# A streaming encoder layer on one core: the sums of x in two heads' slots, the row scale's chain behind the heads, and two kinds of transfer on GpSimd's queue

## The chip, the core and the metric

The kernel runs on one core of one Trainium2 chip. The core has a matrix engine (TensorE, called PE in the profile, PEld for its weight loads), a vector engine (DVE), a scalar engine (ACT), GpSimd (POOL), and SP, which here only issues DMAs. Each engine works through its own queue in order; a DMA is issued from the queue of an engine (here SP or POOL, a few from ACT) and is carried out by 16 DMA engines that all queues share. The metric is the device time of one execution in microseconds; lower is better.

## What is computed

One step of one layer, for 512 prompt frames and 64 sample frames, so 576 columns everywhere in the kernel:

```python
hn = rmsnorm(x, g_norm1)
proj = hn @ w_in
q, k, v, gb, gc, hc = jnp.split(proj, [ATTN_W, 2 * ATTN_W, 3 * ATTN_W, 3 * ATTN_W + CONV_CH, 3 * ATTN_W + 2 * CONV_CH], axis=-1)
q = rmsnorm(q.reshape(B, T, N_HEADS, HEAD_DIM), g_q)
k = rmsnorm(k.reshape(B, T, N_HEADS, HEAD_DIM), g_k)
o_attn = stick_breaking_blocks(q, k_all, v_all, P).reshape(B, T, ATTN_W)
u = gc * hc
conv = conv_w[0] * padded[:, 0:T] + conv_w[1] * padded[:, 1:T + 1] + conv_w[2] * padded[:, 2:T + 2]
o_conv = gb * conv
mix = jnp.concatenate([rmsnorm(o_attn, g_attn_out), rmsnorm(o_conv, g_conv_out)], axis=-1)
x = x + mix @ w_out
h2 = rmsnorm(x, g_norm2)
x = x + (jax.nn.silu(h2 @ w_gate) * (h2 @ w_up)) @ w_down
```

The model width is 2048, there are 8 heads of 128, 8 convolution groups of 128 channels, and the feed-forward width is 5632. The outputs are y, the new keys and values, and the new convolution state, all in 32-bit floats.

## The kernel before

Everything is kept with channels on the 128 partitions and the 576 frames along the free axis, in two halves of 288. A product of 32-bit precision is three matmuls: each operand is split into a high part (a cast, ScalarE, line 223 or 176) and a low part (a subtraction, VectorE, line 224 or 177), and high x high, low x high and high x low are added up in PSUM.

**The order of the work.** TensorE's order is the written one (`tc.manual_schedule`, line 111). The orders of the other engines' queues, SP's and POOL's among them, are made by the framework's planner, except at the start and in the last feed-forward part, where they are the written ones too. Work that has to come between other work is a generator in `pipe` (class `Pipeline`, line 66): each k-step of a product, three matmuls, is one tick, and `yield n` lets a generator sleep for n ticks. `flush` runs all that is left, without any spacing.

**The heads.** `head(h)` projects q, k and v for a head (six products of 16 k-steps, 96 ticks) and spawns the norms, the attention and at its end `put_mix`, which splits a half of the head's output, adds its squares to `acc_a` on GpSimd and stores high and low part to `mix_dram`. The eight outputs lie in `o_attn`, one slot of 576 columns a head.

**The sums of x.** The convolution's inner products, six of eight groups, use a scheme with seven products in place of eight, and need sums of blocks of the scaled x. `x_sums` (line 526), spawned behind head 0, makes them during the heads: for each of 8 pairs j of k-blocks it loads x from `xt_dram` into the slots of heads 6 and 7, which are not used yet, scales and combines four quarters into the slots of heads 4 and 5, and stores the four results in two puts: each put splits two of them into the one buffer `xs_out` and stores both to `xs_dram`, with 8 ticks between the puts of a pair. A pair takes 20 + 3 + 8 + 8 + 8 = 47 ticks, eight pairs 376.

**The row scale.** `group_scale` (line 514) turns the summed squares of the heads, `acc_a`, into the scale by which the first half of the output projection is multiplied: for each half a split, two matmuls with ones (`ssg`, lines 468 and 469), then `rsqrt_mean`. It is spawned at the end of the last head's `attend` with a delay of 4 ticks.

**Stage B.** `open_b` (line 782) is called when the third product of the first convolution group has its first half; it flushes all generators, frees the heads' tiles and starts to load three of the four sums into `bt["pool"]`'s tiles `t1` to `t3`. Two groups run as plain products, the other six in 9 calls of seven products (`conv_run`), each operand prepared four products ahead (`conv_prepare`). The two halves of a group's output go through `put_mix` as well, into places 8 to 15 of `mix_dram`. In the last call, product 6 is the last to read tile `t1` and product 7 the last to read `t2`; behind each, one half of the heads' `mix_dram` is loaded into the freed tile as `ma[0]` and `ma[1]` (line 983). Products 5, 3 and 4 of that call follow, then the output projection: for each of 16 row blocks and both halves, 8 k-steps over the heads (`pjo`), first half 0 and then half 1, so `ma[0]` and then `ma[1]` are read whole within the first two products. Each weight block of 1024 KB is loaded and split ahead of its use (`load_weight`, `split_weight`), and the 16 blocks of x, 288 KB each, are loaded for the residual. Then come the convolution groups' half, and the feed-forward part.

The launch reserves 1024 bytes per partition for GpSimd's DMAs (`dynamic_dma_scratch_size=1024`, line 1626). Before the change POOL's queue issues DMAs only late in the kernel: 7 stores of `hid_dram` and 32 loads of the residual that accumulate (line 1508).

Of the kernel before, what the change touches and what calls it, by code (L numbers as in the profile page):

```python
# [10 lines left out]
F32 = mybir.dt.float32  # L11
F32R = mybir.dt.float32r
AF = mybir.ActivationFunctionType
ALU = mybir.AluOpType
# [6 lines left out]
HALF = T // 2  # L21
# [3 lines left out]
NH = 8  # L25
# [69 lines left out]
def tile_hybrid_stream_step(  # L95
# [6 lines left out]
    nc = tc.nc  # L102
# [21 lines left out]
    xt_dram = tc.dram_tile([KD, P, T], F32, name="xt_dram")  # L124
# [3 lines left out]
    xs_dram = tc.dram_tile([4, NP, 2, P, HALF], F32, name="xs_dram")  # L128
    mix_dram = tc.dram_tile([2, KD, 2, P, HALF], F32, name="mix_dram")
# [79 lines left out]
    pipe = Pipeline()  # L209
# [12 lines left out]
    def split(hi, lo, src, lo_eng=None):  # L222
        nc.scalar.copy(out=hi, in_=src)  # L223
        (lo_eng or nc.vector).tensor_tensor(out=lo, in0=src, in1=hi.bitcast(F32), op=ALU.subtract)  # L224
# [35 lines left out]
    def misc(name):  # L260
        return ps_z.tile([P, 512], F32, tag="misc", name=name, bufs=2)
# [40 lines left out]
    o_attn = apool.tile([P, NH, T], F32, tag="oa", name="o_attn")  # L302
# [69 lines left out]
    with tc.manual_schedule(engines={mybir.EngineType.Activation, mybir.EngineType.DVE, mybir.EngineType.SP}):  # L372
        raw, raw3, src = weight_raw(0)
# [25 lines left out]
        for kt in range(KD + LAG):  # L399
# [66 lines left out]
    def channel_sums(src_hi, src_lo, a, b, name):  # L466
# [33 lines left out]
    def put_mix(k, i, src, gcol, acc, first):  # L500

        t = tmp.tile([P, 2, HALF], F32R, tag="hl", name="mx")
        nc.scalar.activation(out=t[:, 0], in_=src, func=AF.Copy, scale=gcol)
        if first:
            nc.scalar.activation(out=acc, in_=src, func=AF.Square)
        else:
            sq = tmp.tile([P, HALF], F32, tag="sq", name="sqm")
            nc.scalar.activation(out=sq, in_=src, func=AF.Square)
            nc.gpsimd.tensor_tensor(out=acc, in0=acc, in1=sq, op=ALU.add)
        nc.vector.scalar_tensor_tensor(out=t[:, 1], in0=src, scalar=gcol, in1=t[:, 0].bitcast(F32),  # L510
                                       op0=ALU.mult, op1=ALU.subtract)
        nc.sync.dma_start(out=mix_dram[i, k].rearrange("f p t -> p f t"), in_=t.bitcast(F32))

    def group_scale(acc, dst, rows_of):

        for a, b in HALVES:
            sh, sl = parts("sqg")
            split(sh, sl, acc[:, a:b])
            yield rows_of
            ss = channel_sums(sh, sl, a, b, "ssg")  # L520
            rsqrt_mean(dst[:, a:b], ss, 8 * P, HALF)
            yield rows_of

    acc_a = rpool.tile([P, T], F32, tag="R", name="acc_a", bufs=2)

    def x_sums():


        for j in range(NP):
            raw = o_attn[:, 6:8, :]  # L530
            nc.sync.dma_start(out=raw, in_=xt_dram[2 * j : 2 * j + 2].rearrange("k p t -> p k t"))
            yield 20
            ev, od = raw[:, 0, :], raw[:, 1, :]
            ge, go = g1c[:, 2 * j : 2 * j + 1], g1c[:, 2 * j + 1 : 2 * j + 2]
            ta, tb = (o_attn[:, q, :].rearrange("p (q t) -> p q t", q=2) for q in (4, 5))
            b11, b22 = tb[:, 0], ta[:, 1]
            nc.scalar.activation(out=b11, in_=ev[:, :HALF], func=AF.Copy, scale=ge)
            nc.scalar.activation(out=b22, in_=od[:, HALF:], func=AF.Copy, scale=go)
            nc.vector.scalar_tensor_tensor(out=ta[:, 0], in0=ev[:, HALF:], scalar=ge, in1=b11,
                                           op0=ALU.mult, op1=ALU.subtract)  # L540
            nc.vector.scalar_tensor_tensor(out=tb[:, 0], in0=ev[:, HALF:], scalar=ge, in1=b22,
                                           op0=ALU.mult, op1=ALU.subtract)
            yield 3
            nc.vector.tensor_tensor(out=ta[:, 1], in0=b22, in1=ta[:, 0], op=ALU.subtract)
            nc.vector.scalar_tensor_tensor(out=tb[:, 1], in0=od[:, :HALF], scalar=go, in1=ta[:, 1],
                                           op0=ALU.mult, op1=ALU.subtract)
            for q, two in ((0, ta), (2, tb)):
                yield 8
                split(xs_out[:, :, 0, :], xs_out[:, :, 1, :], two)
                for r in range(2):  # L550
                    nc.sync.dma_start(out=xs_dram[q + r, j].rearrange("f p t -> p f t"), in_=xs_out[:, r].bitcast(F32))
            yield 8

    lags = [0]

# [45 lines left out]
    def attend(h, st):  # L601
# [78 lines left out]
        yield 16  # L680
        vtok, vh, vl = st["vtok"], st["vh"], st["vl"]
        po = misc("po")
        mm(po[:, 384:512], vtok[:, 3, :], pb[3], start=True, stop=False, skip_group_check=True)
        for i in (2, 1, 0):
            for n, (a_, b_) in enumerate(((vh, ph[i]), (vl, ph[i]), (vh, pl[i]))):
# [10 lines left out]
        for b in (2, 1, 0):  # L696
            nc.gpsimd.tensor_tensor(out=sums[:, b * TS : (b + 1) * TS], in0=sums[:, (b + 1) * TS : (b + 2) * TS],
                                    in1=sp[:, (b + 1) * TS : (b + 2) * TS], op=ALU.add)
# [11 lines left out]
                                       op0=ALU.min, op1=ALU.add)  # L710
# [7 lines left out]
        for i, (a, b) in enumerate(HALVES):  # L718
            yield 3
            put_mix(h, i, o_attn[:, h, a:b], col("ga", h), acc_a[:, a:b], h == 0)  # L720
        if h == NH - 1:
            pipe.spawn(group_scale(acc_a, acc_a, 30), 4)

    def values(h, st, Ev):
        yield 5
# [56 lines left out]
    def open_b():  # L782

        pipe.flush()
        t1.release()
        bt["pool"] = bpool = tc.alloc_tile_pool(name="bpool", bufs=1, reuse_waits="tile", side="left")
        for q in (1, 2, 3):
            t = bt[q] = bpool.tile([P, NP, 2, HALF], F32R, tag=f"t{q}", name=f"xs_t{q}")
            nc.sync.dma_start(out=t.bitcast(F32), in_=xs_dram[q].rearrange("j f p t -> p j f t"))
        cx = apool.tile([P, NH * T], F32, tag="oa", name="cx")  # L790
        bt["raw"] = cx[:, :2048]
        bt["s1"] = cx[:, 2048:3072].rearrange("p (j c) -> p j c", c=P)
        bt["c"] = cx[:, 3072 : 3072 + UW - 2]
        bt["acc"] = cx[:, 3072 + UW : 3072 + UW + T]

    uc = cpool.tile([P, UC], F32, tag="uc", name="uc")
    u = uc[:, :UW]
# [177 lines left out]
    ma = {}  # L975
    for k_, (n, p_) in enumerate(corder):
        conv_run(n, p_)
        if k_ + 4 < len(corder):
            conv_prepare(*corder[k_ + 4])
        if n == len(CU) - 1 and p_ in (6, 7):  # L980
            i = p_ - 6
            ma[i] = bt["pool"].tile([P, NH, 2, HALF], F32R, tag=f"t{p_ - 5}", name=f"mixa{i}")
            nc.sync.dma_start(out=ma[i].bitcast(F32), in_=mix_dram[i, :NH].rearrange("k f p t -> p k f t"))
        if k_ in (len(corder) - 6, len(corder) - 4):
            load_weight()
        if k_ == len(corder) - 3:
            split_weight(nc.vector)
# [651 lines left out]
```

## Time and profile before

| | us |
|---|---|
| median of 3 runs | 2419.79 |
| lowest, highest | 2417.83, 2422.32 |
| the profiled execution | 2421.78 |
| its span | 2420.1 |

| stage (from the timeline) | about, us |
|---|---|
| turning x, start of head 0 | 0 to 45 |
| heads | 45 to 465 |
| convolution groups, plain and in calls | 430 to 716 |
| output projection | 717 to 924 |
| first feed-forward block | 924 to 999 |
| gate and up | 999 to 1900 |
| down | 1900 to 2420 |

The profiled execution's own time stands 1.99 us above the median. A row of a view by stretches gives the stretch, its length, the busy time and instructions of each engine, the clock that TensorE was granted, the share of the DMA engines' time, and GB/s. A timeline row gives the start, how long, the engine and line, the operation, output and inputs, and in brackets the idle time before and what ended it. A waits row gives who waited for whom, the sum of the waits, their number and the longest. In the list of DMA issues the last number is the median time from issue to landing.

### The profile page before, as it was taken

How to read it: one execution, taken by the hardware profiler on the slowest of the kernel's cores; microseconds unless marked ns; L12 is line 12 of the kernel's file. 1: busy time of each engine (PE TensorE's matmuls, PEld its weight loads, DVE VectorE, ACT ScalarE, POOL GpSimd, SP SyncE). 2: the span in 40 equal slices, each digit the busy share in tenths (PEclk: the TensorE clock that was granted, in tenths of full speed). 3: DMA queues.
4: the chain of work that ended last, by engine and by line, in shares of the span. 5: the costliest groups of instructions: out<-in, count | busy, mean ns of one | idle time of the engine just before them, and what ended most of it. 6: DMA issues, size and time to landing. Idle time of an engine off the chain costs nothing.

```text
span 2420.1 us, 44077 instructions
## 1 busy us (share of the span) xinstructions
PE 2389.3 (99%) x17921; PEld 2376.1 (98%) x17921; DVE 1865.9 (77%) x2810; ACT 1137.6 (47%) x2015; POOL 236.2 (10%) x336
## 2 busy tenths in 40 slices
PE   8999999999999999999999999999999999999999
PEld 8999999999999999999999999999999999999999
DVE  7877666568875567888888888888888777887876
ACT  6666655424442245444444444444444444444444
POOL 1111111100100020000000000000000001431211
PEclk9999999999999999999999999999999999999999
DMA  8555333554357342553444444434534945885542
GB/s 282 167 173 163 92 93 104 175 161 125 92 193 251 98 136 90 154 159 117 151 149 139 134 144 149 145 124 154 159 114 155 323 148 179 235 234 194 196 134 80
DMA packets 500739, 378.96 MB, mean 157 GB/s; under 512 B 11582, under 2 KB 490680, under 8 KB 500536
## 3 DMA queue, kind: packets, MB, share of 16 engines
q1 hardware_dynamic: 494648, 369.04, 47.7%
q0 software_dynamic: 5168, 6.79, 1.6%
q8 instruction: 140, 2.29, 0.4%
q14 instruction: 63, 0.52, 0.1%
q10 hardware_dynamic: 720, 0.33, 0.0%
HBM read 292.93 MB, written 83.18 MB: 155 GB/s over the span
## 4 chain that ended last, share of the span: by engine, by line
PE 87%; DVE 5%; DMA 4%; ACT 3%; issue 1%; POOL 0%; SPq 0%; ACTq 0%; POOLq 0%; DVEq 0%
PE psy L1389 32%; PE psw L1389 16%; PE pj L214 10%; PE pjo L214 8%; PE psx L1389 8%; PE psy L910 5%; PE psw L910 2%; PE pw L1232 2%; PE psx L910 1%; DMA xs_dram<-xs_out 1%; DVE wlo L177 1%; DMA mixa<-mix_dram 1%; DVE whl L224 1%; DMA raw_a<-in_w_in_dram 1%; DMA o_attn<-xt_dram 0%
## 5 line engine op out<-in xcount | busy, mean ns | idle before, releaser
L1389 PE MATMUL psy<-t,whl 128*128 128x288 f32 x2916 | 437.9, 295 | 0.0
L1389 PE MATMUL psy<-h_s,whl 128*128 128x288 f32 x2724 | 411.3, 295 | 2.7 <-ACT part L1399 2.7
L224 DVE TENSOR_TENSOR whl<-raw_a,whl 128x1024 fp32r<-128x1024 f32 (+4 forms) x324 | 355.9, 1100 | 66.9 <-ACT whl L223 66.0
L1389 PEld LDWEIGHTS psy<-t,whl 128*128 128x128 f32 x2916 | 403.3, 188 | 0.2
L214 PE MATMUL pj<-x,whi 128*128 128x288 f32 x1856 | 401.3, 301 | 0.3 <-DVE x L355 0.3
L1389 PEld LDWEIGHTS psy<-h_s,whl 128*128 128x128 f32 x2724 | 377.8, 188 | 3.5 <-ACT part L1399 3.4
L1389 PE MATMUL psw<-t,whl 128*128 128x288 f32 x2592 | 376.8, 295 | 0.0
L223 ACT CAST whl<-raw_a 128x1024 fp32r<-128x1024 f32 (+4 forms) x324 | 296.8, 919 | 164.6 <-issue 38.7
L1389 PEld LDWEIGHTS psw<-t,whl 128*128 128x128 f32 x2592 | 354.0, 188 | 0.2
L214 PEld LDWEIGHTS pj<-x,whi 128*128 128x128 f32 x1856 | 309.8, 191 | 1.1 <-DVE x L355 0.7
L214 PE MATMUL pj<-x,wlo 128*128 128x288 f32 x928 | 276.3, 298 | 0.1
L224 DVE TENSOR_TENSOR whl<-raw_b,whl 128x1024 fp32r<-128x1024 f32 (+5 forms) x186 | 193.9, 1043 | 68.9 <-ACT whl L223 68.0
L223 ACT CAST whl<-raw_b 128x1024 fp32r<-128x1024 f32 (+5 forms) x186 | 160.9, 867 | 161.4 <-issue 69.5
L1399 ACT COPY part<-psy 128x288 f32<-128x288 f32 x237 | 94.7, 399 | 268.4 <-PE psy L1389 268.1
L214 PEld LDWEIGHTS pj<-x,wlo 128*128 128x128 f32 x928 | 176.9, 191 | 0.7 <-DVE wlo L422 0.3
L1389 PE MATMUL psx<-h_s,whl 128*128 128x288 f32 x1122 | 165.1, 295 | 0.2 <-DVE gs L1212 0.2
L1389 PEld LDWEIGHTS psx<-h_s,whl 128*128 128x128 f32 x1122 | 154.2, 188 | 0.4 <-ACT form L223 0.4
L176 ACT CAST whi<-raw_a 128x1024 fp32r<-128x1024 f32 (+1 forms) x101 | 101.7, 1028 | 95.5 <-PE pjo L214 64.2
L177 DVE TENSOR_TENSOR wlo<-raw_a,whi 128x1024 fp32r<-128x1024 f32 (+1 forms) x96 | 119.6, 1264 | 8.7 <-ACT whi L176 5.5
L223 ACT CAST whl<-s 128x1024 fp32r<-128x1024 f32 (+5 forms) x79 | 70.1, 887 | 98.7 <-PE psw L1389 97.2
L214 PE MATMUL pjo<-mixa,whi 128*128 128x288 f32 x512 | 102.6, 295 | 2.9 <-DMA mixa<-mix_dram 2.9
L214 PE MATMUL pjo<-mixc,whi 128*128 128x288 f32 x512 | 101.7, 294 | 0.0
(421 smaller groups left out, 3885.6 us busy)
## 6 DMA issues: line engine op xcount, KB each, us to landing
hid_dram<-form SPq DMA_DIRECT2D x147, 288.0 KB, 2.6
raw_a<-in_w_in_dram SPq DMA_DIRECT2D x41, 1024.0 KB, 5.5
raw_a<-in_w_gate_dram SPq DMA_DIRECT2D x23, 1024.0 KB, 5.3
raw_a<-in_w_up_dram SPq DMA_DIRECT2D x23, 1024.0 KB, 5.5
raw_b<-in_w_gate_dram SPq DMA_DIRECT2D x21, 1024.0 KB, 7.2
raw_b<-in_w_up_dram SPq DMA_DIRECT2D x21, 1024.0 KB, 6.4
h_s<-hid_dram SPq DMA_DIRECT2D x10, 2016.0 KB, 9.8
raw_a<-in_w_out_dram SPq DMA_DIRECT2D x16, 1024.0 KB, 5.1
```

Source lines behind the costliest of these rows:

```text
L176: nc.scalar.copy(out=hi[:, a:b], in_=raw[:, a:b])
L177: lo_eng.tensor_tensor(out=lo[:, a:b], in0=raw[:, a:b], in1=hi[:, a:b].bitcast(F32), op=ALU.subtract)
L214: mm(ps, w_[:, k, csl], x_, start=(k == 0 and n == 0), stop=(k == nk - 1 and n == 2))
L223: nc.scalar.copy(out=hi, in_=src)
L224: (lo_eng or nc.vector).tensor_tensor(out=lo, in0=src, in1=hi.bitcast(F32), op=ALU.subtract)
L910: mm(ps, whl[:, w_, j, :], x_, start=(start and j == 0 and q == 0), stop=(j == NP - 1 and q == 2), skip_group_check=True)
L1232: mm(pss[j, i], w_[:, k, j * P : (j + 1) * P], x_, start=(kk == 0 and k == 0 and n == 0), stop=(kk == 1 and k == 7 and n == 2))
L1389: mm(ps, whl[:, w_, j, :], x_, start=(start and j == 0 and q == 0), stop=(j == len(xs_) - 1 and q == 2), skip_group_check=True)
L1399: nc.scalar.copy(out=t, in_=st["y"])
```

## The change

It has three parts.

1. `x_sums` works in place: the four quarters of a pair are combined in the slots of heads 6 and 7 themselves, one operation every 8 ticks, and the slots of heads 4 and 5 are left alone. The first put stands between the second and the third combination and the second at the end, 24 ticks apart; a pair takes 18 + 7 x 8 = 74 ticks, eight pairs 592. An assertion says that heads 6 and 7 write their slots only after the last pair.
2. `group_scale` for `acc_a` is spawned at the end of `open_b`, behind the flush, instead of at the end of the last head.
3. The convolution groups' stores in `put_mix` go by GpSimd's queue; so do the loads of `ma`, each in four pieces of two heads (576 KB) instead of one load of 2304 KB on SP's queue.

```diff
-        nc.sync.dma_start(out=mix_dram[i, k].rearrange("f p t -> p f t"), in_=t.bitcast(F32))
+        (nc.sync if k < NH else nc.gpsimd).dma_start(out=mix_dram[i, k].rearrange("f p t -> p f t"), in_=t.bitcast(F32))
...
+        four = o_attn[:, 6:8, :].rearrange("p k (i t) -> p (k i) t", i=2)
+        b11, b12, b21, b22 = (four[:, q, :] for q in range(4))
+        stt, tt = nc.vector.scalar_tensor_tensor, nc.vector.tensor_tensor
+        def put(two, names):
+            split(xs_out[:, :, 0, :], xs_out[:, :, 1, :], two)
+            for r, q in enumerate(names):
+                nc.sync.dma_start(out=xs_dram[q, j].rearrange("f p t -> p f t"), in_=xs_out[:, r].bitcast(F32))
         for j in range(NP):
-            raw = o_attn[:, 6:8, :]
-            nc.sync.dma_start(out=raw, in_=xt_dram[2 * j : 2 * j + 2].rearrange("k p t -> p k t"))
-            yield 20
+            nc.sync.dma_start(out=o_attn[:, 6:8, :], in_=xt_dram[2 * j : 2 * j + 2].rearrange("k p t -> p k t"))
+            yield 18
...
-            for q, two in ((0, ta), (2, tb)):
-                yield 8
-                split(xs_out[:, :, 0, :], xs_out[:, :, 1, :], two)
-                for r in range(2):
-                    nc.sync.dma_start(out=xs_dram[q + r, j].rearrange("f p t -> p f t"), in_=xs_out[:, r].bitcast(F32))
+            nc.scalar.activation(out=b11, in_=b11, func=AF.Copy, scale=ge)
+            nc.scalar.activation(out=b22, in_=b22, func=AF.Copy, scale=go)
             yield 8
+            stt(out=b11, in0=b12, scalar=ge, in1=b11, op0=ALU.mult, op1=ALU.subtract)
+            yield 8
+            stt(out=b12, in0=b12, scalar=ge, in1=b22, op0=ALU.mult, op1=ALU.subtract)
+            yield 8
+            put(four[:, 0:2, :], (0, 2))
+            yield 8
+            tt(out=b22, in0=b22, in1=b11, op=ALU.subtract)
+            yield 8
+            stt(out=b21, in0=b21, scalar=go, in1=b22, op0=ALU.mult, op1=ALU.subtract)
+            yield 8
+            put(four[:, 2:4, :], (3, 1))
+            yield 8
+        free_places.append(True)
...
+        assert h < 6 or free_places
...
-        if h == NH - 1:
-            pipe.spawn(group_scale(acc_a, acc_a, 30), 4)
...
         bt["acc"] = cx[:, 3072 + UW : 3072 + UW + T]
+        pipe.spawn(group_scale(acc_a, acc_a, 30), 4)
...
-            nc.sync.dma_start(out=ma[i].bitcast(F32), in_=mix_dram[i, :NH].rearrange("k f p t -> p k f t"))
+            for k in range(0, NH, 2):
+                nc.gpsimd.dma_start(out=ma[i][:, k : k + 2].bitcast(F32),
+                                    in_=mix_dram[i, k : k + 2].rearrange("k f p t -> p k f t"))
```

More of the change, by code (lines that the diff above doesn't have):

```diff
@@ L531, in x_sums @@
-            nc.sync.dma_start(out=raw, in_=xt_dram[2 * j : 2 * j + 2].rearrange("k p t -> p k t"))
-            yield 20
-            ev, od = raw[:, 0, :], raw[:, 1, :]
+            nc.sync.dma_start(out=o_attn[:, 6:8, :], in_=xt_dram[2 * j : 2 * j + 2].rearrange("k p t -> p k t"))
+            yield 18
             ge, go = g1c[:, 2 * j : 2 * j + 1], g1c[:, 2 * j + 1 : 2 * j + 2]
-            ta, tb = (o_attn[:, q, :].rearrange("p (q t) -> p q t", q=2) for q in (4, 5))
-            b11, b22 = tb[:, 0], ta[:, 1]
@@ L537, in x_sums @@
[L537 to L546, printed above, removed]
-            for q, two in ((0, ta), (2, tb)):
-                yield 8
-                split(xs_out[:, :, 0, :], xs_out[:, :, 1, :], two)
-                for r in range(2):
-                    nc.sync.dma_start(out=xs_dram[q + r, j].rearrange("f p t -> p f t"), in_=xs_out[:, r].bitcast(F32))
@@ L554, in tile_hybrid_stream_step @@
+            yield 8
[4 more added lines that the diff above has]
+        free_places.append(True)
+    free_places = []
     lags = [0]
```

## Prediction

> **What bounds the kernel now.** I read the page first, then busy time by stretches, the waits of the matmul queue, and the timelines around each wait.
>
> ```profile
> PE 2389.3 (99%) x17921; PEld 2376.1 (98%) x17921; DVE 1865.9 (77%) x2810; ACT 1137.6 (47%) x2015; POOL 236.2 (10%) x336
> ```
> ```profile
> 145.00:195.00 50.00, 48.93 (x365) 48.12 (x364) 38.06 (x73) 29.82 (x65) 8.47 (x13) 1.00 0.58 181
> 245.00:295.00 50.00, 50.00 (x376) 49.63 (x376) 33.72 (x66) 29.58 (x65) 7.59 (x14) 1.00 0.33 98
> 445.00:470.00 25.00, 22.34 (x161) 21.37 (x160) 11.46 (x20) 10.54 (x20) 4.01 (x13) 1.00 0.46 137
> 470.00:520.00 50.00, 50.00 (x369) 50.00 (x368) 27.07 (x42) 13.90 (x21) 3.67 (x7) 0.97 0.77 256
> 520.00:600.00 80.00, 80.00 (x607) 80.00 (x607) 64.11 (x83) 34.48 (x47) 5.58 (x14) 1.00 0.36 108
> 705.00:740.00 35.00, 31.58 (x235) 30.84 (x234) 20.52 (x38) 9.49 (x17) 2.90 (x4) 1.00 1.01 355
> ```
> ```profile
> 120.00:130.00 10.00, 7.20 (x31) 6.67 (x32) 8.59 (x15) 7.72 (x17) 2.59 (x5) 0.59 0.58 168
> 130.00:140.00 10.00, 10.00 (x72) 10.00 (x72) 3.49 (x8) 4.43 (x10) 0.73 (x1) 0.90 0.63 198
> ```
>
> Columns of the last two fences: stretch, its length, busy time of PE, PEld, DVE, ACT and POOL, granted clock, DMA share, GB/s. TensorE is busy 2389.3 of the 2420.1 us, so nothing off its path matters until it makes it wait, and a cure can win only gaps and slow clock. Three gaps touch the change: the first heads, where the sums of x run (idle in 145 to 195, none in 245 to 295, after the sums); 2.7 us before 470; and 3.4 us around 717. A gap also costs clock: 0.59 and 0.90 over the 20 us after one gap are 4.1 + 1.0 = 5.1 us, and 0.97 over 470 to 520 is 1.5 us.
>
> **Part 1, the sums of x.** The same matmul falls at the same place of each head, so its spacing is the length of a head.
>
> ```profile
> 76.83 0.60 PE L739 MATMUL kc<-ident,cK 128*128 128x128 f32 x4
> 134.96 0.60 PE L739 MATMUL kc<-ident,cK 128*128 128x128 f32 x4
> 238.39 0.60 PE L739 MATMUL kc<-ident,cK 128*128 128x128 f32 x4
> 287.85 0.60 PE L739 MATMUL kc<-ident,cK 128*128 128x128 f32 x4
> ```
> ```profile
> 109.17 6.50 DMA xs_dram<-xs_out
> 115.75 0.69 ACT xs_out L223
> ```
> ```profile
> PE vta L586 <- DVE Ev L768: 2.5, 2, 2.1
> PE pjo L214 <- DMA mixa<-mix_dram: 2.9, 2, 2.4
> PE ssg L468 <- ACT sqg L223: 2.1, 2, 1.5
> ```
> ```profile
> xs_dram<-xs_out SPq DMA_DIRECT2D x32, 288.0 KB, 5.2
> o_attn<-xt_dram SPq DMA_DIRECT2D x8, 576.0 KB, 5.5
> ```
>
> A head without the sums takes 287.85 - 238.39 = 49.46 us. The three before it took 58.13 and 103.43, so 161.56 - 3 x 49.46 = 13.2 us too much. The biggest piece is the stall near 120 with its slow clock. In the chain of waits the second put of a pair found the one `xs_out` buffer still being stored (6.50 us), ScalarE stood before it, and the head's own work queued behind. The two puts lay 8 ticks apart; a tick is 49.46 / 96 = 0.515 us, so 4.1 us against a landing of 5.2. Now they lie 24 ticks apart, 12.4 us, and a pair takes 18 + 7 x 8 = 74 ticks instead of 47: eight pairs are 592 ticks, 6.2 heads. The operations are the same four on VectorE, two on ScalarE and two splits, so no work is removed; the assertion in `attend` issues nothing. VectorE in a quiet head is busy 33.72 of 50; 38.06 with the sums. Spread by 47/74, the extra 4.3 becomes some 2.8, which stays under the 38.06 that left 1.1 us idle. The load gets 18 ticks (9.3 us) instead of 20, against a landing of 5.5; it now waits for the last split of the pair, which ordered SP's queue ahead of it anyway. If this cover goes, ScalarE stands again, now in six heads. Bounds: a gain of 13.2, and a loss of 3 (half the 1.1 us idle in each of the six). I take a gain of **9**: the stall and the clock at 120 (2.1 + 5.1), and about a third of the other 6.
>
> **Part 2, row scale's chain.**
>
> ```profile
> 465.11 0.39 PE L716 MATMUL os<-ws,vtok 128*128 128x128 f32 x2
> 467.02 0.40 PE L468 MATMUL ssg<-sqg,oner 128*128 128x288 f32 x1 [1.52 <-ACT sqg L223]
> 469.60 0.30 PE L214 MATMUL pj<-x,whi 128*128 128x288 f32 x1
> ```
>
> Opening stage B empties the list of pending generators at once, so in TensorE's hand-written order the four sums of `acc_a` stand right behind the last head's `os`, before their splits are made. Spawned after the emptying, each has 30 ticks between its split and its matmuls. From 465.5 (end of `os`) to 469.6 is 4.1 us; the four matmuls come back later at 3.17 / 24 = 0.13 us each (24 take 3.17, rows of part 4), 0.5; so 3.6, and the 1.5 us of slow clock behind it: a gain of **5.1**, bounds 3.0 and 5.1. Its VectorE and ScalarE work falls into 470 to 520, where they are busy 27 and 14 of 50; its result is first used after 717. Were that cover gone, the same 4.1 would only move.
>
> **Part 3, the conv groups' stores by GpSimd.** Sixteen stores leave SP and cost POOL an issue each, 0.73 us (rows below), 12 us on an engine 10% busy. TensorE has no gap in 520 to 600, so nothing can be won. Behind a store that waits for VectorE's low part stand POOL's adds and its clears of `u`; the buffer comes free later, with the next product's high part on ScalarE behind it. I take 0, bounds 0 and 6 (2 us late for each of three pairs of groups).
>
> **Part 4, the output projection's input.** This decides.
>
> ```profile
> 686.50 18.57 SPq L184 DMA_DIRECT2D raw_a<-in_w_out_dram  x2
> 706.93 3.93 SPq L983 DMA_DIRECT2D mixa<-mix_dram  x2
> ```
> ```profile
> 699.91 3.17 PE psy L910 x24
> 703.08 3.17 PE psw L910 x24
> 717.05 0.40 PE L214 MATMUL pjo<-mixa,whi 128*128 128x288 f32 x1 [0.53 <-DMA mixa<-mix_dram]
> ```
> ```profile
> 1922.54 0.73 POOL L1152 DMA_DIRECT2D hid_dram<-acc_ax  x1 [2.66 <-DVE acc_ax L224]
> 1925.16 0.73 POOL L1152 DMA_DIRECT2D hid_dram<-form  x1 [1.90 <-DVE acc_z L1414]
> 1927.45 0.73 POOL L1152 DMA_DIRECT2D hid_dram<-acc_z  x1 [1.56 <-DVE acc_t L1414]
> ...
> 2056.89 2.73 POOL L1508 DMA_DIRECT2D acc<-x_dram  x3
> 2063.33 0.86 POOL L1508 DMA_DIRECT2D acc<-x_dram  x1 [3.71 <-issue]
> ...
> 2112.17 2.64 POOL L1508 DMA_DIRECT2D acc_z<-x_dram  x3
> 2115.74 0.86 POOL L1508 DMA_DIRECT2D acc_z<-x_dram  x1 [0.93 <-issue]
> ```
> ```profile
> hid_dram<-form POOLq DMA_DIRECT2D x3, 288.0 KB, 5.7
> hid_dram<-form SPq DMA_DIRECT2D x147, 288.0 KB, 2.6
> ```
>
> Product 6 ends at 703.1 and frees `mixa0`'s place, product 7 at 706.3 `mixa1`'s; SP reached the two loads only at 706.9, having stood 18.57 us at weight loads. TensorE then waited 2.9 us. On POOL's queue the first load can start 3.9 us sooner. But it becomes eight DMAs of 576 KB, 512 rows of 1152 bytes each. Three stores of 256 rows went out within 5 us, inside a landing of 5.7, so 768 rows can be under way. The fourth of the residual's accumulating DMAs stood in both groups shown, with nothing but "issue" to blame: it went out 6.44 us behind the first in one, 3.57 in the other; I read these as busy and quiet DMA. If an accumulated row counts twice (read and added), four are 4 x 128 x 2 = 1024 rows; two pieces are 1024 rows as well. So I expect **one piece at a time**. A piece then costs what the first of four took to give its place back, 3.57 quiet to 6.44 busy, plus 432 KB more than their 144 KB at 355 GB/s, 1.2: 4.8 to 7.7. From 703 to 740 the loads of x (16 x 288 KB) and of weights compete (share 1.01 in 705 to 740); I take three pieces busy and five quiet, 3 x 7.7 + 5 x 4.8 = 47, so the last lands near 750. TensorE would need it at 716.5 (0.53 before 717.05) + 3.17 + 2.4 = 722: a stall of **28**. Bounds: 43 us (all busy, lands at 765), 9 (3.57 each, lands at 731), and 0. The wait of 2.9 it replaces goes away, and the clock comes back late, 1.5 to 5.1 by the two dips above; I take **3**. While POOL stands before a piece, its adds for the last group and their stores stand too, with ScalarE's squares behind them; that ends with the last piece, and I price it at 0, at most 3.
>
> The Trainium skill, "DMA: Bandwidth & Descriptors", section "Anatomy of one DMA — SWDGE (gpsimd) path", gives 2.0 us plus bytes over 436 GB/s: 3.35 us for a piece, as an estimate eight of them land near 734 and the sum ends at 2418, no change. The rows speak against it under load: 288 KB took 5.7 where it gives 2.7. The same page (sections "Terms" and "The descriptor swizzle") has 16-byte descriptors in rings, one more than the rows per engine; with the launch's 1024 bytes that is 64, and two pieces of 33 would not fit, which agrees with the fourth accumulation's wait.
>
> **The sum**, against the profiled execution's own 2421.78 (span 2420.1): -9 - 5.1 - 2.9 + 28 + 3 = +14.0, 2435.8. The median of the runs shown is 2.0 lower, so **2434**.
>
> **Rivals.** (a) *The pieces overlap* as the three stores did, nothing stands: the first data some 4 us after the issue (5.7 less the 1.2 that more than half of such a piece takes), then 4608 KB at 355 GB/s, 13.3: landed by about 721, in time. For it: the three stores. Against it: the fourth accumulation. -9 - 5.1 - 2.9 = -17, 2403: faster, and the deciding point is whether the second piece is issued before the first lands. (b) *One at a time, but quick*, 3.57 each: 9 + 3 - 17 = -5, 2415 (2419 with half the gain of part 1). For it: the quiet rows. Against it: the DMA share of 1.01. (c) *The spread sums do not help*: ScalarE's waits for loads take the place of its wait for `xs_out`, +3 instead of -9, with all pieces busy: 43 + 3 + 3 - 8 = +41, 2461. For it: VectorE's load per head hardly falls. Against: the stall near 120 hangs on the buffer.
>
> **Chances.** Forecast 0.55, (a) 0.23, (b) 0.12, (c) 0.10. A measurement here tells 0.2%, 4.8 us. Faster: (a) and a third of (b), 0.27; within: the rest of (b) and a little of the forecast, 0.11; slower 0.62. The range 2402 to 2455 holds (a), (b), the forecast and the near edge of (c); the forecast's own is 2423 to 2447.
>
> **What would show it.** Right: POOL's timeline has eight issues some 5 to 8 us apart after product 6; TensorE waits for `mixa` over 20 us, then runs at half clock; no `ssg` wait before 470; heads 1 to 3 near 50 us. Wrong: issues about 1 us apart, a `mixa` wait under 3 us, or heads 4 to 6 longer than 49.46. Only TensorE's order is the written one; the other engines' orders are made anew by the framework's planner, and a piece or an add set elsewhere in POOL's queue would shift all this.

## The result, and the profile after

| | median, us | lowest to highest | runs |
|---|---|---|---|
| before, on the same chip | 2420.68 | 2417.83 to 2422.32 | 4 |
| after | 2440.15 | 2438.64 to 2442.28 | 4 |

The ratio is 1.0082 [1.0065, 1.0100]: slower, by some 20 us. The profiled execution took 2438.64 us, its span is 2436.9. From the page of the changed kernel, the busy time of each engine:

```profile
PE 2388.7 (98%) x17921; PEld 2375.9 (97%) x17921; DVE 1864.2 (76%) x2810; ACT 1137.5 (47%) x2015; POOL 260.3 (11%) x360
```

TensorE has the same 17921 matmuls and nearly the same busy time, 2388.7 against 2389.3, so in sum the 16.8 us of the longer span are time in which it stood. (A slow clock lengthens busy time; here the 5.1 and 1.5 us of it that the prediction counts in the kernel before have gone, and some 7.8 are new in the projection, worked out below, so that they nearly cancel.) The waits of its queue say what it stood for (who waits for whom: us in total, times, longest):

```profile
PE pjo L214 <- DMA mixa<-mix_dram: 26.6, 7, 6.2
```

The waits of `vta` for the first heads' row work and of `ssg` for its splits have gone. The wait for the output projection's input, 2.9 us before, is 26.6 now. POOL's timeline shows why; a row has start, length, line, operation, and in brackets what it waited for:

```profile
692.93 0.78 POOL L991 DMA_DIRECT2D mixa<-mix_dram  x1 [0.20 <-issue]
694.19 0.71 POOL L512 DMA_DIRECT2D mix_dram<-mx  x1 [0.49 <-DVE mx L510]
699.86 0.79 POOL L991 DMA_DIRECT2D mixa<-mix_dram  x1 [4.96 <-issue]
707.55 0.76 POOL L991 DMA_DIRECT2D mixa<-mix_dram  x1 [6.90 <-issue]
714.79 0.75 POOL L991 DMA_DIRECT2D mixa<-mix_dram  x1 [6.48 <-DMA x<-xt_dram]
...
732.25 0.76 POOL L991 DMA_DIRECT2D mixa<-mix_dram  x1 [6.04 <-issue]
736.69 0.75 POOL L991 DMA_DIRECT2D mixa<-mix_dram  x1 [3.67 <-issue]
```

Eight issues from 692.93 to 736.69 are 43.76 / 7 = 6.25 us apart on average, and before each of the last seven the engine stood several microseconds: in six cases with "issue" as its only releaser and in one (714.79) with a load of x as the releaser that the profile names. The list of DMA issues (queue, count, KB, median us to landing) has the time that one takes:

```profile
mixa<-mix_dram POOLq DMA_DIRECT2D x8, 576.0 KB, 6.0
mix_dram<-mx POOLq DMA_DIRECT2D x16, 288.0 KB, 2.6
```

A piece lands 6.0 us after its issue at the median, and the next goes out when it has landed: TensorE, which waited for the same piece, goes on at 707.26 and 714.53 (rows below), and GpSimd issues the next one at 707.55 and 714.79, each time less than 0.3 us later. The add of a convolution group that stands behind the last piece runs only at 737.45. On TensorE the products go on piece by piece, and the windows (columns as in the prediction) show the standing and the slow clock:

```profile
707.26 0.40 PE L214 MATMUL pjo<-mixa,whi 128*128 128x288 f32 x1 [3.19 <-DMA mixa<-mix_dram]
714.53 0.61 PE L214 MATMUL pjo<-mixa,whi 128*128 128x288 f32 x1 [6.21 <-DMA mixa<-mix_dram]
```
```profile
445.00:470.00 25.00, 25.00 (x192) 25.00 (x192) 11.21 (x20) 8.68 (x16) 3.29 (x8) 1.00 0.69 227
700.00:740.00 40.00, 14.38 (x68) 12.08 (x66) 6.41 (x12) 4.22 (x8) 7.45 (x10) 0.61 0.76 272
740.00:800.00 60.00, 58.99 (x428) 58.99 (x429) 30.41 (x55) 11.20 (x15) 2.28 (x3) 0.95 0.50 166
```

In 700 to 740 TensorE is busy 14.38 of 40 us at 0.61 of its clock; in 445 to 470, where it was busy 22.34 of 25, it has no gap left. To divide the span I take the same matmul in both timelines: `kc` of the last head, the first product of the convolution calls (`psy<-x`), the first and the last `pjo<-mixa`. The marks in the changed kernel, then the tile view's row for the projection's first half (it has the first and last time), before and after:

```profile
378.00 0.60 PE L745 MATMUL kc<-ident,cK 128*128 128x128 f32 x4
501.55 3.33 PE L917 MATMUL psy<-x,whl 128*128 128x288 f32 x24
```
```profile
L214 PE MATMUL pjo<-mixa,whi x512: 292/294/402, 717.1 to 821.9; 128*128 128x288 f32 x171
```
```profile
L214 PE MATMUL pjo<-mixa,whi x512: 292/294/607, 703.1 to 839.9; 128*128 128x288 f32 x171
```

And the same two marks before:

```profile
386.77 0.60 PE L739 MATMUL kc<-ident,cK 128*128 128x128 f32 x4
515.58 3.33 PE L910 MATMUL psy<-x,whl 128*128 128x288 f32 x24
```

| stretch | before | after | difference |
|---|---|---|---|
| start to the last head's `kc` | 386.77 | 378.00 | -8.8 |
| to the first product of the calls | 128.81 | 123.55 | -5.3 |
| the calls, to the first `pjo<-mixa` | 201.5 | 201.6 | +0.1 |
| the projection's first half | 104.8 | 136.8 | +32.0 |
| the rest | 1598.2 | 1597.0 | -1.2 |

Parts 1 and 2 bring 14.1 us by these marks, the input costs 32.0. Of the 32.0, the waits are 26.6 - 2.4 = 24.2 (one of the 2.9 before, 0.53, lies ahead of the first matmul); the other 7.8 I put down to the slow clock.

### The profile page after: what moved, and what is told of

Read it like the earlier page. It is cut to its first block, busy times and chain, and to the rows that moved or that the text cites. A ratio compares the mean times of both kernels' runs of the same rounds, so it can differ in the third digit from the quotient of the medians.

```text
span 2436.9 us, 44113 instructions
## 1 busy us (share of the span) xinstructions
PE 2388.7 (98%) x17921; PEld 2375.9 (97%) x17921; DVE 1864.2 (76%) x2810; ACT 1137.5 (47%) x2015; POOL 260.3 (11%) x360
## 4 chain that ended last, share of the span: by engine, by line
PE 83%; DVE 8%; DMA 4%; issue 3%; ACT 2%; POOL 1%; SPq 0%; ACTq 0%; DVEq 0%; POOLq 0%
PE psy L1398 32%; PE psw L1398 16%; PE pj L214 12%; PE pjo L214 8%; PE psx L1398 8%; DVE whl L224 2%; PE pw L1241 2%; PE psy L917 1%; DMA raw_a<-in_w_in_dram 1%; PE z L627 0%; DMA cx<-in_w_in_dram 0%; DVE wlo L177 0%; DMA xs_dram<-xs_out 0%; PE pot L1555 0%; PE psw L917 0%
## 5 line engine op out<-in xcount | busy, mean ns | idle before, releaser
L214 PE MATMUL pjo<-mixa,whi 128*128 128x288 f32 x512 | 109.6, 306 | 26.6 <-DMA mixa<-mix_dram 26.6
L214 PEld LDWEIGHTS pjo<-mixa,whi 128*128 128x128 f32 x512 | 87.2, 198 | 28.9 <-DMA mixa<-mix_dram 28.8
```

What stands on the lines that cost most here:

```text
L214: mm(ps, w_[:, k, csl], x_, start=(k == 0 and n == 0), stop=(k == nk - 1 and n == 2))
```

## The experiments

A table at the end of this section has every median and ratio, each against the kernel before on the same chip. The runs were made on three chips, on which that kernel's median was 2420.55 (the input and the pieces by SP, more room, one-head pieces), 2421.30 (the three parts undone, the input by ScalarE) and 2419.06 (the pieces alone, the three gates), so across these groups the ratios are the fairer comparison. What the prediction calls parts 3 and 4 are the two halves of the change's third part, the stores and the input. My theory: parts 1 and 2 gain, GpSimd takes the eight pieces one at a time, and that alone makes the kernel slower.

**The input back on SP, the rest of the change kept.**

```diff
-            for k in range(0, NH, 2):
-                nc.gpsimd.dma_start(out=ma[i][:, k : k + 2].bitcast(F32),
-                                    in_=mix_dram[i, k : k + 2].rearrange("k f p t -> p k f t"))
+            nc.sync.dma_start(out=ma[i].bitcast(F32), in_=mix_dram[i, :NH].rearrange("k f p t -> p k f t"))
```

> The output projection's input goes back to SP's queue as two whole loads; all else is the changed kernel. Theory (the eight pieces on GpSimd's queue go one at a time and cost 26.6 us of waits plus the half clock, 34 us in all): TensorE waits some 3 us for mixa as before, and the time is 2440.2 - 34.2 + 2.9 = 2409, that is 12 under the kernel before. Rival (the queue does not matter, the loads of x that compete for the DMA engines do): about 2440.

Measured 2414.44, ratio 0.9973 [0.9962, 0.9983]: faster than before, and 25.7 us under the changed kernel. The waits and SP's timeline:

```profile
PE pjo L214 <- DMA mixa<-mix_dram: 4.9, 2, 3.7
```
```profile
694.18 5.83 SPq L990 DMA_DIRECT2D mixa<-mix_dram  x2
700.75 20.62 SPq L1018 DMA_DIRECT2D x<-xt_dram  x16
```

The way of the input is the cause of the loss. But it is 5 us above what I expected, and the wait is 4.9 instead of 2.9, although SP issues the two loads from 694.18, when TensorE wants the input at 705.1. SP still stood at the weight loads first, as before the change, and reached the first load 2.5 us after product 6 had freed its tile. That remainder is followed up below.

**The eight pieces, but by SP.** This separates the cutting into pieces from the queue: the kernel of the change, with the loop kept.

```diff
-                nc.gpsimd.dma_start(out=ma[i][:, k : k + 2].bitcast(F32),
+                nc.sync.dma_start(out=ma[i][:, k : k + 2].bitcast(F32),
```

> The changed kernel with the same eight pieces of two heads, on SP's queue. Theory (the queue is what costs, not the cutting): as with the two whole loads on SP within 2 us, about 2409. Rival (the cutting costs, each piece's fixed time adds up): over 2415, with waits for mixa of 8 us and more.

Measured 2413.68, 0.9969 [0.9957, 0.9981]. SP issued all eight within 10.75 us, and the wait is that of two whole loads:

```profile
694.54 10.75 SPq L991 DMA_DIRECT2D mixa<-mix_dram  x8
```
```profile
PE pjo L214 <- DMA mixa<-mix_dram: 3.2, 2, 2.0
```

The pieces cost nothing on SP's queue; it is GpSimd's queue that makes them one at a time.

**More room for GpSimd's DMAs.** If a second piece waits for room in what the launch reserves for GpSimd's DMAs, a little more should let two go out together; the 128 bytes come from a pad that shrinks.

```diff
-    rpad.tile([P, 56], F32, name="rpad_t")
+    rpad.tile([P, 24], F32, name="rpad_t")
...
-    nc = _bacc.Bacc("TRN2", target_bir_lowering=False, num_devices=1, dynamic_dma_scratch_size=1024)
+    nc = _bacc.Bacc("TRN2", target_bir_lowering=False, num_devices=1, dynamic_dma_scratch_size=1152)
```

> The changed kernel with 1152 reserved bytes per partition for GpSimd's DMAs instead of 1024, and 128 bytes less of an unused pad, nothing else. Theory (a limit on what may be under way, 64 descriptors of 16 bytes per DMA engine in 1024 bytes, 33 for a piece): 1152 bytes hold 72, two pieces of 33 fit, so the second piece is issued about 1 us after the first and the third waits for the first; at 3 to 3.5 us a piece the last lands near 720 instead of 741, the waits for mixa fall to some 11 us and the time to about 2421. Rival (GpSimd starts a load only when the one before has landed, whatever the room): pieces 4.4 to 7.7 us apart as now, 2440.

Measured 2436.66, 1.0063 [1.0049, 1.0076]: 3.5 us better instead of some 20. POOL's timeline and the list of its DMA issues:

```profile
707.62 1.54 POOL L991 DMA_DIRECT2D mixa<-mix_dram  x2 [5.17 <-issue]
716.04 0.75 POOL L991 DMA_DIRECT2D mixa<-mix_dram  x1 [6.88 <-issue]
718.29 0.76 POOL L991 DMA_DIRECT2D mixa<-mix_dram  x1 [1.50 <-issue]
```
```profile
mixa<-mix_dram POOLq DMA_DIRECT2D x8, 576.0 KB, 7.7
```
```profile
PE pjo L214 <- DMA mixa<-mix_dram: 16.4, 7, 4.7
```

The room is what GpSimd stood for: with 128 bytes more, two pieces go out 0.8 us apart, and there are two under way from then on. I had expected a wait of some 11 us and 2421. It goes from 26.6 to 16.4 only: two under way take 7.7 us each at the median instead of 6.0. From the first issue to the end of TensorE's last wait the eight pieces take 38.0 us instead of 48.1. The median follows by 3.5 us rather than 10. In the profiles, the projection's first half does take 9.9 us less (126.9 against 136.8), but TensorE came to it 7.0 us later than in the changed kernel, 4.8 of them from the heads (their spread is a subject below). Whether the edit itself causes that was not tried.

**Pieces of one head.** The same total in 16 pieces of 288 KB.

```diff
-            for k in range(0, NH, 2):
-                nc.gpsimd.dma_start(out=ma[i][:, k : k + 2].bitcast(F32),
+            for k in range(NH):
+                nc.gpsimd.dma_start(out=ma[i][:, k : k + 1].bitcast(F32),
```

> The changed kernel with sixteen pieces of one head (288 KB, 256 rows) on GpSimd's queue instead of eight of two. Theory (a limit on rows under way; 17 descriptors a piece, three fit in 64): three are issued in a row, the fourth waits for the first, some 2 us a piece, the last lands near 729, the waits fall to about 20 us, time about 2431. Rival (each load waits for the one before, whatever its size): sixteen times some 5 us, the last lands near 775, time about 2475.

Measured 2427.11, 1.0030 [1.0021, 1.0039], 13 us better than the changed kernel and 4 better than expected. POOL's timeline:

```profile
693.96 0.73 POOL L991 DMA_DIRECT2D mixa<-mix_dram  x1 [0.15 <-issue]
695.26 0.73 POOL L512 DMA_DIRECT2D mix_dram<-mx  x1 [0.57 <-DVE mx L510]
695.99 0.73 POOL L991 DMA_DIRECT2D mixa<-mix_dram  x1
699.56 2.30 POOL L991 DMA_DIRECT2D mixa<-mix_dram  x3 [2.85 <-issue]
```
```profile
PE pjo L214 <- DMA mixa<-mix_dram: 12.8, 12, 2.0
```

A piece, a store and a piece go out within 2 us, then the engine stands: three transfers of 256 rows fit, as the three stores in the prediction did, where a store and one of 512 rows fill the room. With the room filled more evenly, the last piece goes out 12.1 us sooner (724.55 against 736.69). The limit goes by the size of the transfers under way (rows or bytes, which these runs do not tell apart), not by their number.

**The pieces alone.** Part 4 put into the kernel before, with nothing else of the change.

```diff
-            nc.sync.dma_start(out=ma[i].bitcast(F32), in_=mix_dram[i, :NH].rearrange("k f p t -> p k f t"))
+            for k in range(0, NH, 2):
+                nc.gpsimd.dma_start(out=ma[i][:, k : k + 2].bitcast(F32),
+                                    in_=mix_dram[i, k : k + 2].rearrange("k f p t -> p k f t"))
```

> The kernel before with part 4 alone: the eight pieces on GpSimd's queue, all else as before. Theory (the parts add up; the pieces cost 34.2 us against 2.4 of waiting in their stage): 2420.7 + 29 to 32, about 2450. Rival (the pieces are slow only because the moved stores stand between them and the loads of x start early): under 2440.

Measured 2453.54, 1.0141 [1.0125, 1.0157]: +34.5 us. Part 4 does not need the other parts to cost what it does; its wait is

```profile
PE pjo L214 <- DMA mixa<-mix_dram: 30.4, 7, 6.7
```

These 34.5 us are more than the 25.7 between the changed kernel and the one with the input by SP. In the profiles, the projection's first half takes 140.5 us here, 136.8 in the changed kernel, 108.5 with the input by SP and 104.8 before: 35.7 against 28.3, so most of the difference lies in this stage, and half of it is what the input by SP still costs more than before.

**Undoing parts 1, 2 and 3, each in the kernel with the input on SP.** Three kernels, each the one with two whole loads on SP and one of these edits:

```diff
     def x_sums():
...
-            yield 18
+            yield 20
...
-            put(four[:, 2:4, :], (3, 1))
+            for q, two in ((0, ta), (2, tb)):
+                yield 8
+                split(xs_out[:, :, 0, :], xs_out[:, :, 1, :], two)
```
```diff
+        if h == NH - 1:
+            pipe.spawn(group_scale(acc_a, acc_a, 30), 4)
...
-        pipe.spawn(group_scale(acc_a, acc_a, 30), 4)
```
```diff
-        (nc.sync if k < NH else nc.gpsimd).dma_start(out=mix_dram[i, k].rearrange("f p t -> p f t"), in_=t.bitcast(F32))
+        nc.sync.dma_start(out=mix_dram[i, k].rearrange("f p t -> p f t"), in_=t.bitcast(F32))
```

> The kernel with the input on SP's queue (2414.4), and the sums of x as before the change: scratch in the slots of heads 4 and 5, puts 8 ticks apart. Theory (the spread sums end the stalls of the first heads; the last head's mark came 6.8 us earlier in the profile of the kernel with the input on SP than before): 2414.4 + 6.8 = 2421, with heads 1 to 3 together 13 us over three quiet heads of 49.46. Rival (the heads' gain comes from the newly planned order of the other queues, not from the sums): 2414 to 2416.

> The kernel with the input on SP's queue (2414.4), and the row scale's chain spawned at the last head's end as before the change. Theory: TensorE waits for ssg again, 3.6 us, and runs 1.5 us behind at half clock: 2414.4 + 5.1 = 2419.5. Rival (the gap is filled by what the earlier heads left, since the heads now end sooner): 2414 to 2416.

> The kernel with the input on SP's queue (2414.4), and the convolution groups' stores on SP's queue as before the change. Theory (nothing in the calls waits for them, so they cost and win nothing there): 2414.4 within 1. Rival (they held SP up before the two loads of the input: 706.9 against the end of product 7 at 706.3 before, 694.2 against 694.9 with the stores on GpSimd): about 1.5 us more, 2416.

*Old sums*: 2417.20, 0.9985 [0.9975, 0.9995], 2.8 us above the kernel with part 1, with overlapping intervals: between what the theory and what the rival had expected. The 2.1 us wait of the first heads is back:

```profile
PE vta L586 <- DVE Ev L766: 2.1, 1, 2.1
```

but its profile has the clock at 1.00 over 115 to 145, where the kernel before had 0.83 (windows of that stretch, first before, then here):

```profile
115.00:145.00 30.00, 26.67 (x171) 25.83 (x170) 19.59 (x40) 20.33 (x43) 3.54 (x7) 0.83 0.52 161
```
```profile
115.00:145.00 30.00, 27.20 (x204) 26.51 (x204) 21.15 (x42) 21.19 (x45) 4.00 (x7) 1.00 0.52 162
```

So the same wait brought a slow clock in one execution and none in another. The third profile with the old sums, that of the pieces alone, has the wait too (2.1 us) and a clock of 0.89 over this stretch. In the two with a slow clock a gap of 0.5 us stands some 2 us ahead of the wait, which the third lacks; whether that matters isn't shown. The `kc` of the last head shows how far this reaches; the latest with the new sums (more room), then the earliest with the old ones (this kernel):

```profile
382.77 0.60 PE L745 MATMUL kc<-ident,cK 128*128 128x128 f32 x4
```
```profile
383.12 0.60 PE L737 MATMUL kc<-ident,cK 128*128 128x128 f32 x4
```

With the new sums the eleven profiles have it from 377.34 to 382.77, median 378.78; with the old ones three have 383.12, 386.77 and 389.41 (the pieces alone). No two overlap, and the medians are 8.0 apart; yet the medians of the runs are only 2.8 apart. A part of this spread lies ahead of the second head's `kc`. Counted from there, the eleven take 301.1 to 303.5 us (median 301.4) and the three 305.0 (this kernel), 309.0 and 309.9, so against that median the old sums cost 3.6 in this kernel's profile and 7.6 and 8.5 in the other two. Its eleven runs also lie 8.7 us apart, against 3.6 for the eight of the kernel with the input on SP. That part 1 gains is shown; whether it is 3 or 8 in a typical execution isn't settled.

*Old row scale*: 2417.72, 0.9986 [0.9978, 0.9995], 3.3 us above, the intervals overlapping again, and again between theory and rival. Its profile answers more sharply: `ssg` waits 2.1 us, and from the last head's `kc` (377.84) to the first product of the calls (507.74) it takes 129.9 us, against 123.6 in the kernel with part 2.

```profile
PE ssg L468 <- ACT sqg L223: 2.1, 2, 1.5
```
```profile
377.84 0.60 PE L747 MATMUL kc<-ident,cK 128*128 128x128 f32 x4
507.74 3.33 PE L918 MATMUL psy<-x,whl 128*128 128x288 f32 x24
```

*Old stores*, which is parts 1 and 2 alone: 2411.10, 0.9958 [0.9946, 0.9971]. This is 3.3 us *below* the kernel with the stores on GpSimd, on another chip and with intervals that just overlap; the pair with a gate on x below, on one chip, confirms it (2408.71 against 2412.90, no run of one within the other's range). So part 3, which I had put at nothing, costs. SP's timeline shows what differs:

```profile
695.80 4.45 SPq L990 DMA_DIRECT2D mixa<-mix_dram  x2
704.19 2.80 SPq L512 DMA_DIRECT2D mix_dram<-mx  x2
707.09 1.64 SPq L1018 DMA_DIRECT2D x<-xt_dram  x3
```
```profile
PE pjo L214 <- DMA mixa<-mix_dram: 3.2, 2, 2.4
```

Here the loads of x start at 707.09, because SP stands at the last group's stores first; without these stores it starts them at 700.75, while the input is still on its way. The windows of 700 to 720, first with the stores on GpSimd and then on SP, show a DMA share of about 1 in both and TensorE busier in the second:

```profile
700.00:720.00 20.00, 15.14 (x96) 14.64 (x95) 10.05 (x19) 5.50 (x11) 4.40 (x6) 0.83 1.06 400
```
```profile
700.00:720.00 20.00, 16.83 (x113) 16.32 (x113) 10.78 (x21) 5.51 (x11) 2.49 (x3) 0.91 1.04 371
```

So I read it thus: the stores that stood on SP had held back other transfers, to the input's advantage. The kernel with eight pieces by SP fits this: its stores are on GpSimd, but the pieces keep SP busy until 705.39, when x starts, and its wait is 3.2 as here. That this is the whole way is argued, not shown.

**The input's loads elsewhere, and x behind them.** If x beside the input is the cost, then x should wait for it, and an earlier issue of the input should help. Two edits: the two whole loads on ScalarE's queue (an edit of the kernel with the input on SP), and a gate on x (all but its first two blocks): a copy of one column that reads the end of `ma[1]`, and that the load of x then overwrites. The gate was put into parts 1 and 2 alone, into the kernel with the input on SP, and into the one with it on ScalarE.

```diff
-            nc.sync.dma_start(out=ma[i].bitcast(F32), in_=mix_dram[i, :NH].rearrange("k f p t -> p k f t"))
+            nc.scalar.dma_start(out=ma[i].bitcast(F32), in_=mix_dram[i, :NH].rearrange("k f p t -> p k f t"))
```
```diff
+    for j in range(1, NP):
+        nc.gpsimd.tensor_copy(x2t[j][:, :, 0], ma[1][:, NH - 1, :, HALF - 1].bitcast(F32))
```

> The changed kernel with the output projection's input as two whole loads on ScalarE's queue. With the input on SP's queue TensorE still waited 4.9 us and ran 6.83 us at half clock, for SP stands at a weight load until 694.2, 2.5 us after product 6 has freed the first tile. Theory (ScalarE's queue is free there): the first load starts at the end of product 6, the waits fall to about 1 us and the dip goes: 2414.4 - 7 = 2407. Rival (the second load, which can start only with the end of product 7, and the DMA engines' rate set the wait): 2412 to 2415. Second rival (ScalarE standing for products 6 and 7 holds up its casts): waits for whl or part in the products behind, over 2415.

> The kernel with the first two parts of the change alone (2411.1: sums, chain; input and stores on SP's queue), and the loads of x, but the first two, made to wait for the input: GpSimd copies one column of the second input tile into each x tile before the load. Theory (loads of x that run beside the input lengthen it; here SP stood at two stores anyway until 707, so it is shielded already): 2411 within 2, the waits for mixa some 3 us as they were. Rival (the delay of x makes the output projection's additions late): over 2414.

> The kernel with the input on SP's queue and the stores on GpSimd's (2414.4), and the loads of x behind the input as in the other run. Theory (the stores' move cost 3.3 us only because SP no longer stood at them, and the loads of x began at 700.8 beside the input): the waits for mixa fall from 4.9 to about 3 and the time to 2411. Rival (the stores on GpSimd's queue cost by themselves): 2414.

> The kernel with the input on ScalarE's queue (2415.3), and the loads of x behind the input. Theory (the two loads begin with products 6 and 7 done, but share the DMA engines with the loads of x that began at 700.2): alone they are 4608 KB at 355 GB/s, 13.3 us, from about 690 to 703.5 and so in time for their products; the wait of 7.9 falls to under 2 and the time to 2407. Rival (the weight load that SP issues ahead, or the DMA engines' own rate, sets it): 2412 and more.

ScalarE's queue gave 2415.32 and 2414.64 with the gate, no better than SP, where I had expected 2407. It issues the two loads at 690.02 and 692.43, within a microsecond of their tiles being free, while SP sends weight loads and x; TensorE's wait for the input is longer, in one piece:

```profile
PE pjo L214 <- DMA mixa<-mix_dram: 7.9, 1, 7.9
```

That is the ungated one; with the gate it is 7.1. The gate on the kernel with the stores on GpSimd gave 2412.90 against 2414.44, not separable, with the wait still 4.9: SP now sent two blocks of x and a weight load of 1024 KB into the same stretch instead.

```profile
698.93 6.21 SPq L1020 DMA_DIRECT2D x<-xt_dram  x2
705.25 0.48 SPq L184 DMA_DIRECT2D raw_a<-in_w_out_dram  x1
```

So the gate on x does not remove this wait, and it does not show x to be what lengthens it: something else took x's place. What is left fits the DMA engines' rate: in parts 1 and 2 alone, the weight load and the 4608 KB input, 5632 KB, at the 355 GB/s of 705 to 740 take 16.2 us from about 695, which ends near 711. This is an estimate; that the remaining wait can't be had by any order was not tried. With the gate on parts 1 and 2 alone the time is 2408.71, 0.9952 [0.9937, 0.9967], with a wait of 2.6: the lowest of the study, but by the ratios not separable from the same kernel without the gate.

**All of them.**

| kernel | median, us | ratio to before | runs |
|---|---|---|---|
| the change | 2440.15 | 1.0082 [1.0065, 1.0100] | 4 |
| input by SP, whole | 2414.44 | 0.9973 [0.9962, 0.9983] | 8 |
| input by SP, eight pieces | 2413.68 | 0.9969 [0.9957, 0.9981] | 5 |
| more room for GpSimd | 2436.66 | 1.0063 [1.0049, 1.0076] | 4 |
| one-head pieces | 2427.11 | 1.0030 [1.0021, 1.0039] | 10 |
| pieces alone | 2453.54 | 1.0141 [1.0125, 1.0157] | 4 |
| input by SP, old sums | 2417.20 | 0.9985 [0.9975, 0.9995] | 11 |
| input by SP, old row scale | 2417.72 | 0.9986 [0.9978, 0.9995] | 11 |
| parts 1 and 2 alone | 2411.10 | 0.9958 [0.9946, 0.9971] | 5 |
| input by ScalarE | 2415.32 | 0.9974 [0.9965, 0.9983] | 10 |
| parts 1 and 2, x gated | 2408.71 | 0.9952 [0.9937, 0.9967] | 4 |
| input by SP, x gated | 2412.90 | 0.9971 [0.9959, 0.9982] | 7 |
| input by ScalarE, x gated | 2414.64 | 0.9982 [0.9971, 0.9992] | 8 |

## Why the prediction was right, step by step

The forecast was 2434 and the time is 2440.15, slower as forecast and inside the likeliest case's own range. Its mechanism held: pieces one at a time, "some 5 to 8 us apart" (4.4 to 7.7 measured), a wait of over 20 us, half clock (0.50 over 720 to 740), no `ssg` wait. The sum is nearer than its terms: by the medians, parts 1 and 2 alone bring 10.2 rather than 14.1 and the input alone costs 34.5 rather than 28.1, so the measured parts do not simply add up to the 19.5 of the change. That the error stayed at 6 us owes something to luck.

- **Part 1, -9.** The marks say -8.8; heads 1 to 3 take 52.1, 51.4 and 49.5 us, near 50 as foreseen, and the next three 49.46 each, as a quiet head. The stall at 120 is gone, and so is its slow clock; but the clock's 5.1 us, which I booked as a sure part of the term, does not come with every execution of the old sums (two of three profiles have a slow clock), and undoing the part costs only 2.8 by the medians. The term was probably too large for the median, by something that stays open.
- **Part 2, -5.1.** The marks say -5.3. Undone, 6.3 by the marks and 3.3 by the medians. The sums of `acc_a` found their cover in 470 to 520, where TensorE is busy 50.00 of 50 us at a clock of 1.00.
- **Part 3, 0 (bounds 0 and 6).** It costs 3.3 where the input is on SP, inside the bounds, but the mechanism that I bounded (a buffer freed late on POOL) does not show: the calls take 201.6 us against 201.5. The step that failed: I asked what the stores would meet on POOL's queue, not what they had held back on SP's, where x now starts 6.3 us sooner. In the changed kernel itself the input doesn't run on SP, and what part 3 costs there was not measured.
- **The old `mixa` wait, -2.9.** Right for the changed kernel, where it became part of the new one. In the kernels with the input on SP it stayed, at 2.6 to 4.9. I had read SP's late arrival at 706.9 as its cause. The runs on SP don't cure that: SP's loads and TensorE's need moved together, and SP's first load was 9.5 to 11.4 us ahead of the need, against 9.6 before. ScalarE's queue issues earlier, and there the wait grew to 7.9. So an earlier issue alone does not end the wait; that the load of the DMA engines sets it is my estimate above, not shown.
- **Part 4, +28 for the stall, +3 for the clock.** The stall is 26.6, from pieces 6.25 us apart against the (3 x 7.7 + 5 x 4.8) / 8 = 5.9 that I took; TensorE needed the input from 703 on, not from 717, since it had gained 14, and the first piece went out at 692.93, not 703. The clock was mis-sized: 7.8 instead of 3, because I took the dips of single gaps of 2 to 3 us, where seven gaps kept it at 0.61 for 40 us and 0.95 for 60 more. Worked out in the same way, it is 7.7 in the pieces alone, 8.1 with more room and 7.5 with one-head pieces, so it hardly follows the sum of the waits (30.4, 16.4 and 12.8 us).
- **The rivals.** That the pieces overlap (2403) fell with the issue times. "One at a time, but quick" (2415) fell as well: 4.4 us is the shortest gap. With more room the pieces do overlap, and it isn't 2403 then either, but 2436.66.

The estimate of the room that the prediction worked out from the page "DMA: Bandwidth & Descriptors" of the Trainium skill (sections "Terms" and "The descriptor swizzle": 16-byte descriptors, one more than the rows of each engine), 64 descriptors where two pieces want 66, is borne out: with 1152 bytes, by the same estimate 72, two fit and go out together. The rule for the time of a DMA in its section "Anatomy of one DMA — SWDGE (gpsimd) path" gives 3.35 us for a piece, as an estimate; the trace has 6.0. (Eight of these from 703 end near 730, not the 734 of the prediction, and the sum by it at 2414, not 2418; the prediction doesn't hang on it.)

## What to carry to other kernels

A transfer that is moved to another queue takes its price from that queue, not from the old one: the same eight pieces cost nothing on SP and 26 us on GpSimd, which stood before each until the one before had landed and given back its room. Before large transfers go to such a queue, look in the trace for the place where it stands with "issue" as its only releaser, and count the rows that were under way. And ask of every instruction that leaves a queue what it had held back there: here, with the stores gone, SP sent x 6.3 us sooner and beside the input, and the kernel lost 3.3 us.

## What the hardware showed unexpectedly

What a short gap costs in clock can't be read from one execution. TensorE's gap before the projection's second half is 2.40 us in the kernel before and 2.41 in parts 1 and 2 alone, and in the 6 us ahead of its end TensorE is busy 3.59 and 3.60 us. The windows behind it (before, then parts 1 and 2 alone) have the clock at 1.00 in one and at 0.90 in the other:

```profile
723.00:740.00 17.00, 16.96 (x128) 16.96 (x129) 7.42 (x17) 2.29 (x5) 0.00 (x0) 1.00 1.01 355
```
```profile
712.00:729.00 17.00, 16.97 (x116) 16.97 (x117) 5.95 (x14) 2.29 (x5) 0.00 (x0) 0.90 0.99 353
```

GpSimd's 288 KB stores of the convolution groups land in 2.6 us at the median, as SP's stores of `hid_dram` do in the kernel before (SP's of `mix_dram` took 3.7 there), so a single transfer isn't slow for its queue alone. Two 576 KB pieces under way took 7.7 us each at the median where one took 6.0, so the eight gained 10 of 48 us, not half. Seven to twelve gaps within some 25 to 40 us cost 7.5 to 8.1 us of clock beyond the gaps themselves.
